# A hybrid decoder layer on one core: the forms of h made at later tiles, and the last group's output stores issued by SP

## Chip, cores and metric

One core of one Trainium2 chip. The metric is the device time of one execution in microseconds. Before the change it is 947.24 us, the median of 3 runs (946.95 to 947.94).

## What is computed

One decoder layer over 512 tokens of width 2048, in float32:

```python
h = rms_norm(x, norm_gain)
z = h @ w_in
q, k, v, g_attn, c_b, c_c, c_h, g_conv = split(z)
y_attn = sliding_window_attention(rope(norm(q)), rope(norm(k)), v, sinks) * silu(g_attn)
y_conv = c_b * short_conv(c_c * c_h, conv_w) * silu(g_conv)
x = x + concat(y_attn, y_conv) @ w_out
gate = sigmoid(rms_norm(x, ple_gate_norm_gain) @ w_ple_gate + b_ple_gate)
e = rms_norm(p @ w_ple_proj, ple_norm_gain)
return x + gate * e
```

Attention has 16 query heads and 4 key heads of 64, in blocks of 128 tokens; the convolution has three taps.

## The kernel before, in words

Every float32 operand of a matmul is split into an upper part (a cast to fp32r on ACT) and the remainder (a subtraction on DVE), and each product is made of three matmuls: upper by upper, remainder by upper, upper by remainder (`mm3`, L154; names end in h and l).

**First stage.** k and v come first (L268 to L284), from 16 tiles of x as they arrive. Then `product` (L514) is called for tiles numbered from 0: tiles 0 to 7 are q, tiles 8 to 14 alternate c and h of the convolution (8 c, 9 h, 10 c, 11 h, 12 c, 13 h, 14 c); one last h tile follows at L1283. A tile is one `gemm_tile` (L165): 16 steps k of three matmuls each, with a weight split fetched every four. After every second k it calls `tick` (L144), which runs what was set with `at(when, ...)` for that count. So the small PE work (sums over heads, transposes, attention's scores, transposes and values) is put between the matmuls at fixed places: `token_rstd` (L233) puts the sum of x's squares at c0+3, the transposes of its copy (`take_rows`, L208, the tile rowsum; `to_tokens`, L213) at c0+5, and the spreading of the result rb at c0+8, c0 being the start of tile 0; the sums of k's squares stand at c0+6, and those of q tile t mostly six ticks after its end. Tiles 2 to 5 also hold an `e_block` (L543), the projection of p, in their middle. Attention's 16 cells are spread over tiles 6 to 14.

In this stage only PE's order is the code's own (L53). The orders of ACT, DVE, POOL and SP are chosen when the kernel is built, from the program's order and estimated times; each of them then runs in that fixed order. The tiles tagged "big" (31 buffers) hold x, squares, rotated heads, rowsum, and the tiles of the forms.

**The forms of h.** The second stage multiplies 2 x 2 blocks by sums of blocks, a scheme of seven products per block. `h_forms(j)` (L646), for j from 0 to 7, makes for the pair of tiles 2j, 2j+1 of h those sums that are not plain blocks: it loads two tiles of x again (L650, through SP; the tile xg), scales each by the norm gain on ACT (L651), makes four half-width sums on DVE (L604, L605, L611, L612; the tile g), splits them with ACT and DVE (L585, L586; the tiles hf) and stores the four results to DRAM through POOL's queue (L654; h_dram). In the second stage `bring` (L1313) loads them back through SP. `load_p` (L533) loads p and splits it (ptsh, ptsl) ahead of tile 0.

`busy` maps a tile's number to functions that `product` calls after that tile's matmuls have been issued (L519). Before the change, `h_forms(0)` is called ahead of tile 0 and `h_forms(1)` to `h_forms(7)` after the tiles 0, 1, 2, 3, 6, 9 and 12.

**Later stages.** Eight groups g of 28 steps on PE, each step 12 matmuls at L854. Here the orders of all engines are the code's own (L706): `soon(before | after, s, fn)` hangs work on a step. The weights of the first steps (wx, wy, loaded by `load_more`, L765, through SP) use the room of the "big" tiles, so their loads wait for these. Groups 6 and 7 are the gate. In `gate_group` (L1152), `finish(t, n, s)` (L1198) puts the sigmoid after step s, the product with e and the accumulating load of x2 (`add_x2`, L1192, through POOL) after s + 1, and `store` (L1195) after s + 5: the output of 128 x 2 x 512 values, 512 KB, through POOL's queue. In group 7 two quarters go this way, (0, 1) with the store after step s0 + 25 and (1, 1) after s0 + 26; the other two are stored in pieces of 256 and 128 KB by `piece` (L1239), through SP, from step s0 + 25 to the end.

Of the kernel before, what the change touches and what calls it, by code (L numbers as in the profile page):

```python
# [30 lines left out]
def f32(ap):  # L31
    return ap.bitcast(F32)
# [3 lines left out]
def hymba_layer(ctx: ExitStack, tc: tile.TileContext, io):  # L36
# [14 lines left out]
    nc = tc.nc  # L51
# [253 lines left out]
    with ExitStack() as att:  # L305
# [218 lines left out]
        def btile(name):  # L524
            return big.tile([P, T], F32, tag="big", name=name)
# [7 lines left out]
        def load_p():  # L533
            load_pg(0)
            for k in range(2):
                pt = btile("pt")
                nc.gpsimd.dma_start(pt, io["p"][k])
                pts.append(split_tile(pt, name="pts"))
# [107 lines left out]
        def h_forms(j):  # L646
            raw = []
            for k in (2 * j, 2 * j + 1):
                raw.append(btile("xg"))
                nc.sync.dma_start(raw[-1], io["x"][k])  # L650
                nc.scalar.activation(raw[-1], raw[-1], AF.Copy, scale=norm_g[:, k : k + 1])  # L651
            _, work = make_forms(
                raw, lambda: btile("g"), lambda: (None, big.tile([P, 2, 2 * P], F32R, tag="big", name="hf")),
                sink=lambda i, t: nc.gpsimd.dma_start(h_dram[j][i], f32(t.rearrange("p a b -> p (a b)"))),  # L654
            )
            for piece in ("g57", "g63", "5", "63", "7"):
                work[piece]()

        load_p()
        h_forms(0)  # L660
        for j, i in enumerate((0, 1, 2, 3, 6, 9, 12), 1):
            busy.setdefault(i, []).append(lambda j=j: h_forms(j))
        for u in range(NKV * NB):
            attention(u // NB, u % NB, c0 + (51 + 7 * u if u < 2 else 65 + 46 * (u - 2) // 13))
# [80 lines left out]
    for g in range(NG):  # L745
        w, n = groups[g]
# [313 lines left out]
    def part(ap, t, n):  # L1060
        return ap[:, 2 * t : 2 * t + 2, n * T : (n + 1) * T]
# [88 lines left out]
    out = io["out"].rearrange("b p n -> p b n")  # L1150

    def gate_group(g):  # L1152
        s0 = g * PER
        q, ext = {}, {}
# [38 lines left out]
            nc.gpsimd.dma_start(q[t, n], x2_dram[t][2 * (g - 6) + n], accum_op=ALU.add)  # L1193

        def store(t, n):  # L1195
            nc.gpsimd.dma_start(part(out, t, 2 * (g - 6) + n), q[t, n])

        def finish(t, n, s):  # L1198
            soon(after, s, sigmoid, t, n)
            for b in range(2):  # L1200
                soon(after, s + 1, times_e, t, n, b)
            soon(after, s + 1, add_x2, t, n)
            soon(after, s + 5, store, t, n)
# [192 lines left out]
def build(arrays):  # L1396
    import concourse.bacc as bacc

    nc = bacc.Bacc("TRN2", target_bir_lowering=False, num_devices=1)
    io = {  # L1400
        n: nc.dram_tensor(f"in_{n}", v.shape, mybir.dt.from_np(v.dtype), kind="ExternalInput").ap()
        for n, v in arrays.items()
    }
    io["out"] = nc.dram_tensor("out_t", (NB, P, D), F32, kind="ExternalOutput").ap()
    with tile.TileContext(nc) as tc:
        hymba_layer(tc, io)
    return nc
# [9 lines left out]
```

## Time and profile before

| what | value |
|---|---|
| median of 3 runs | 947.24 us |
| the profiled execution | 947.18 us |
| its span, first to last instruction | 945.4 us |
| PE busy | 924.7 us (98%) |
| DVE busy | 740.2 us (78%) |
| ACT busy | 535.8 us (57%) |
| POOL busy | 147.4 us (16%) |
| mean granted TensorE clock | 0.992 |

The profile is one execution recorded on the chip. PE is TensorE's matmuls and PEld its weight loads, DVE is VectorE, ACT ScalarE, POOL GpSimd, SP SyncE, which issues DMAs. In rows in order of time the columns are the start and the duration in us, engine, line, operation, output <- inputs and the count; a bracket gives the time that the engine sat idle before it and what it waited for. Matmuls are pipelined, so their starts, not their durations, tell the rate. In tables by stretches PEclk is the granted clock as a share of full speed.

### The profile page before, as it was taken

Reading aid. Unit: us, or ns where it says so; the run is one execution under the profiler, and the core shown is the slowest. Engines: PE = TensorE matmul, PEld = TensorE weight load, DVE = VectorE, ACT = ScalarE, POOL = GpSimd, SP = SyncE. Lnnn points to the kernel's source line nnn. Section 1 sums busy time; section 2 is a strip of 40 time slices with the busy share of each in tenths; the row PEclk is TensorE's granted clock in tenths of the full one; section 3 lists DMA queues with packets and bytes.
Section 4 is the critical chain, followed back from the end, with each engine's and each line's share of the span. In section 5 each row is a group of like instructions: output and inputs, shape, how many; then the busy total and the mean of one; then the engine's idle time right before and its main releaser. Section 6 shows DMA issues by size and latency. Waiting matters only on the chain.

```text
span 945.4 us, 12287 instructions
## 1 busy us (share of the span) xinstructions
PE 924.7 (98%) x4264; PEld 767.8 (81%) x4264; DVE 740.2 (78%) x1115; ACT 535.8 (57%) x890; POOL 147.4 (16%) x192
## 2 busy tenths in 40 slices
PE   9959999999999999999999999999999999999997
PEld 8848878888888888888888888888888888888885
DVE  6756898897786667677767778989767796999778
ACT  7634766777775344445444436655566676575452
POOL 2012224134232000100100020010120112001101
PEclk9979999999999999999999999999999999999999
DMA  8543676436567866734933888794996996578747
GB/s 313 178 153 134 222 245 210 135 92 162 109 179 229 303 223 192 166 108 148 255 90 131 238 237 240 246 265 110 282 346 198 223 282 164 133 228 271 180 135 211
DMA packets 68334, 188.22 MB, mean 199 GB/s; under 512 B 8144, under 2 KB 14592, under 8 KB 68272
## 3 DMA queue, kind: packets, MB, share of 16 engines
q1 hardware_dynamic: 46768, 129.52, 40.1%
q0 software_dynamic: 21360, 57.91, 26.6%
q8 instruction: 33, 0.54, 0.2%
q14 instruction: 29, 0.24, 0.1%
q10 hardware_dynamic: 144, 0.01, 0.0%
HBM read 158.05 MB, written 29.36 MB: 198 GB/s over the span
## 4 chain that ended last, share of the span: by engine, by line
PE 94%; DVE 3%; issue 1%; DMA 1%; ACT 1%; SPq 0%; DVEq 0%; ACTq 0%
PE psp L854 59%; PE psg L155 6%; PE psg L156 6%; PE psg L157 6%; PE pst L854 3%; PE pss L276 2%; PE pst L276 2%; PE pst L920 2%; PE pst L484 1%; PE pss L564 1%; PE pst L564 1%; PE pss L452 1%; PE pss L451 1%; PE pso L499 1%; PE pso L498 1%
## 5 line engine op out<-in xcount | busy, mean ns | idle before, releaser
L854 PE MATMUL psp<-wh,form 128*128 128x512 f32 x1152 | 356.2, 390 | 0.0
L854 PEld LDWEIGHTS psp<-wh,form 128*128 128x128 f32 x1152 | 215.3, 188 | 44.4 <-DVE form L586 0.4
L854 PE MATMUL psp<-wl,form 128*128 128x512 f32 x576 | 224.2, 389 | 0.0
L821 DVE TENSOR_TENSOR wl<-wy,wh 128x1024 fp32r<-128x1024 f32 x96 | 117.1, 1221 | 53.1 <-ACT wh L820 52.3
L820 ACT CAST wh<-wy 128x1024 fp32r<-128x1024 f32 x96 | 100.8, 1051 | 92.5 <-PE psp L854 72.7
L854 PEld LDWEIGHTS psp<-wl,form 128*128 128x128 f32 x576 | 108.1, 188 | 22.5
L820 ACT CAST wh<-ws 128x1024 fp32r<-128x1024 f32 x64 | 67.5, 1054 | 71.4 <-PE psp L854 48.5
L821 DVE TENSOR_TENSOR wl<-wx,wh 128x1024 fp32r<-128x1024 f32 x64 | 78.3, 1223 | 37.3 <-ACT wh L820 36.9
L820 ACT CAST wh<-wx 128x1024 fp32r<-128x1024 f32 x64 | 67.4, 1052 | 69.4 <-PE psp L854 59.2
L155 PE MATMUL psg<-hsh,wh 128*128 128x512 f32 x256 | 103.1, 403 | 0.0
L156 PE MATMUL psg<-hsl,wh 128*128 128x512 f32 x256 | 100.7, 393 | 0.0
L157 PE MATMUL psg<-hsh,wl 128*128 128x512 f32 x256 | 100.4, 392 | 0.0
L854 PE MATMUL psp<-wh,hsh 128*128 128x512 f32 x256 | 100.0, 391 | 0.0
L854 PE MATMUL psp<-wl,hsh 128*128 128x512 f32 x256 | 99.6, 389 | 0.0
L854 PE MATMUL psp<-wh,hsl 128*128 128x512 f32 x256 | 99.6, 389 | 0.0
L821 DVE TENSOR_TENSOR wl<-ws,wh 128x1024 fp32r<-128x1024 f32 x64 | 78.2, 1222 | 27.0 <-ACT wh L820 26.9
L118 DVE TENSOR_TENSOR wl<-raw,wh 128x512 fp32r<-128x512 f32 x88 | 60.2, 686 | 27.4 <-ACT wh L117 11.2
L806 DVE TENSOR_TENSOR wy<-wy,ws 128x1024 f32<-128x1024 f32 x64 | 77.9, 1217 | 0.0
L117 ACT CAST wh<-raw 128x512 fp32r<-128x512 f32 x88 | 54.1, 616 | 41.7 <-PE psg L156 29.4
L157 PEld LDWEIGHTS psg<-hsh,wl 128*128 128x128 f32 x256 | 48.5, 189 | 10.6
L854 PEld LDWEIGHTS psp<-wl,hsh 128*128 128x128 f32 x256 | 48.1, 188 | 9.9
L854 PEld LDWEIGHTS psp<-wh,hsl 128*128 128x128 f32 x256 | 48.1, 188 | 9.9
(232 smaller groups left out, 1401.4 us busy)
## 6 DMA issues: line engine op xcount, KB each, us to landing
raw<-in_w_in SPq DMA_DIRECT2D x32, 512.0 KB, 3.6
ws<-in_w_mid SPq DMA_DIRECT2D x32, 512.0 KB, 4.3
wx<-in_w_mid SPq DMA_DIRECT2D x20, 512.0 KB, 3.7
h<-hf POOLq DMA_DIRECT2D x32, 256.0 KB, 3.4
wy<-in_w_mid SPq DMA_DIRECT2D x16, 512.0 KB, 7.9
wx<-in_w_out SPq DMA_DIRECT2D x16, 512.0 KB, 6.9
ws<-in_w_out SPq DMA_DIRECT2D x16, 512.0 KB, 5.9
ws<-in_w_ple_gate SPq DMA_DIRECT2D x16, 512.0 KB, 4.4
```

Source lines behind the costliest of these rows:

```text
L117: nc.scalar.copy(wh, raw)
L118: nc.vector.tensor_tensor(wl, raw, f32(wh), op=ALU.subtract)
L155: nc.tensor.matmul(ps, wh, ah, start=first, stop=False)
L156: nc.tensor.matmul(ps, wh, al, start=False, stop=False)
L157: nc.tensor.matmul(ps, wl, ah, start=False, stop=last)
L276: nc.tensor.matmul(kv_ps[t], w[:, t, :], a, start=k == 0 and i == 0, stop=k == KT - 1 and i == 2)
L564: nc.tensor.matmul(banks[t], a, w, start=k == 0 and i == 0, stop=k == 1 and i == 2)
L806: tt(y, y, got[g, "s1" if f == 6 else "s0", c], op=ALU.add)
L820: nc.scalar.copy(wh, src)
L821: tt(wl, src, f32(wh), op=ALU.subtract)
L854: nc.tensor.matmul(ps[t], a, w[:, i], start=start and first and i == 0 and n == 0, stop=last and i == 1 and n == 2, skip_group_check=not s ...
L920: nc.tensor.transpose(pt[:, b], quads[b // 2][:, b % 2, f * P : (f + 1) * P], ident)
```

## The change

`h_forms` is no longer called ahead of tile 0; the eight calls come after the tiles 1, 2, 6, 8, 9, 11, 12 and 13 (q's second, third and seventh tile, and five of the convolution's c and h). And in the last group (g = 7) `store` issues its two output stores through SP's queue instead of POOL's; group 6 stays as it was.

```diff
@@ -657,8 +657,7 @@
         load_p()
-        h_forms(0)
-        for j, i in enumerate((0, 1, 2, 3, 6, 9, 12), 1):
+        for j, i in enumerate((1, 2, 6, 8, 9, 11, 12, 13)):
             busy.setdefault(i, []).append(lambda j=j: h_forms(j))
@@ -1193,7 +1192,8 @@
         def store(t, n):
-            nc.gpsimd.dma_start(part(out, t, 2 * (g - 6) + n), q[t, n])
+            engine = nc.gpsimd if g == 6 else nc.sync
+            engine.dma_start(part(out, t, 2 * (g - 6) + n), q[t, n])
```

## Rows read from the trace of the kernel before

**Rows 1.** The page's first part: busy time, share of the span, instructions.

```profile
PE 924.7 (98%) x4264; PEld 767.8 (81%) x4264; DVE 740.2 (78%) x1115; ACT 535.8 (57%) x890; POOL 147.4 (16%) x192
```

**Rows 2.** PE's waits over the whole span: total us, times, longest.

```profile
PE psm L219 <- ACT rowsum L210: 10.6, 1, 10.6
...
PE pso L205 <- ACT sh L130: 1.0, 1, 1.0
PE pss L451 <- DVE negm L459: 0.7, 1, 0.7
```

**Rows 3.** PE in order of time, 56 to 76 us.

```profile
56.70 0.39 PE L157 MATMUL psg<-hsh,wl 128*128 128x512 f32 x1
67.66 0.58 PE L219 MATMUL psm<-ident,rowsum 2*128 2x2 f32 x4 [10.57 <-ACT rowsum L210]
68.17 0.80 PE L155 MATMUL psg<-hsh,wh 128*128 128x512 f32 x1
...
73.46 0.39 PE L157 MATMUL psg<-hsh,wl 128*128 128x512 f32 x1
...
75.54 0.39 PE L157 MATMUL psg<-hsh,wl 128*128 128x512 f32 x1
```

**Rows 4.** By stretches: us, each engine's busy time, PEclk, DMA share, GB/s.

```profile
60.00:62.00 2.00, 0.00 (x0) 0.00 (x0) 0.00 (x0) 0.00 (x0) 0.00 (x0) 0.50 0.96 363
```

**Rows 5.** ACT in order of time, 56 to 68 us.

```profile
56.05 1.14 ACT L130 CAST ptsh<-pt 128x512 fp32r<-128x512 f32 x2
62.80 0.72 ACT L651 ACTIVATE xg<-xg,norm_gain 128x512 f32<-128x512 f32 x1 [5.61 <-DMA xg<-in_x]
...
67.04 0.57 ACT L210 COPY rowsum<-pso 2x512 f32<-2x512 f32 x1
```

**Rows 6.** SP's issues in order of time: the first four loads of xg.

```profile
58.70 1.85 SPq L650 DMA_DIRECT2D xg<-in_x  x4
```

**Rows 7.** DVE in order of time, 58 to 71 us.

```profile
58.22 1.28 DVE L131 TENSOR_TENSOR ptsl<-pt,ptsh 128x512 fp32r<-128x512 f32 x2
...
68.28 0.17 DVE L243 TENSOR_REDUCE ms<-psm 128x4 f32<-128x8 f32 x1 [0.40 <-PE psm L219]
...
70.03 0.43 DVE L249 COPY rb<-r_x 128x512 f32<-128x512 f32 x1 [1.38 <-POOL r_x L229]
```

**Rows 8.** Groups by line: one of the four sums; the subtractions of all sets.

```profile
L605 DVE TENSOR_TENSOR g<-xg 128x256 f32<-128x256 f32 x8 | 3.4, 422 | 4.4 <-ACT xg L651 4.4
...
L586 DVE TENSOR_TENSOR hf<-g,hf 128x256 fp32r<-128x256 f32 (+1 forms) x24 | 11.6, 510 | 1.6 <-ACT hf L585 1.4
```

**Rows 9.** By stretches: length, then PE, PEld, DVE, ACT, POOL busy, PEclk.

```profile
134.30:154.30 20.00, 18.64 (x85) 14.66 (x84) 18.77 (x35) 13.73 (x31) 7.15 (x9) 1.00 0.60 210
...
196.00:301.00 105.00, 105.00 (x561) 89.25 (x560) 83.05 (x253) 78.36 (x224) 34.31 (x40) 1.00 0.62 167
```

**Rows 10.** ACT in order of time: after tile 1, and after tile 3.

```profile
94.17 1.33 ACT L651 ACTIVATE xg<-xg,norm_gain 128x512 f32<-128x512 f32 x2
...
132.39 0.72 ACT L651 ACTIVATE xg<-xg,norm_gain 128x512 f32<-128x512 f32 x1 [0.46 <-DMA xg<-in_x]
...
137.72 0.61 ACT L130 CAST sh<-sqh 128x512 fp32r<-128x512 f32 x1
```

**Rows 11.** Ahead of the second stage: POOL, SP and ACT in order of time.

```profile
268.50 0.54 POOL L654 DMA_DIRECT2D h<-hf  x1 [0.53 <-DVE hf L586]
...
285.23 1.82 SPq L778 DMA_DIRECT2D wx<-in_w_mid  x4
...
297.65 1.06 ACT L820 CAST wh<-wx 128x1024 fp32r<-128x1024 f32 x1
```

**Rows 12.** The end: POOL's last store, SP's last, and DMA issues (median us to landing).

```profile
936.43 0.74 POOL L1196 DMA_DIRECT2D out_t<-z  x1 [2.98 <-DMA z<-x]
...
941.76 0.33 SPq L1244 DMA_DIRECT2D out_t<-z  x1
...
out_t<-z POOLq DMA_DIRECT2D x2, 512.0 KB, 4.9
```

## The prediction, made before the changed kernel was run

> **What bounds the kernel now.** I read the page's busy times first: PE is busy 924.7 us of a span of 945.4 [rows 1], so only what makes PE stop, or run slowly, is worth anything. The list of PE's waits comes next. In all the span it names few: 10.6 us once, for the copy rowsum at L210, and 1.0 and 0.7 us for a half of a square and for attention's negated maxima [rows 2]. I then read PE's order of time around the long one. The matmul that starts at 56.70 is the last before the gap; the transposes of rowsum start at 67.66 with 10.57 us of idle ahead of them, and the matmuls that follow are slow: from 68.17 to 73.46 there are 12 starts in 5.29 us, while from 73.46 to 75.54 nine take 2.08, or 0.231 each [rows 3]. The table by stretches says why: the granted clock is 0.50 at 60 to 62 us, the lower of the two levels, 1.2 instead of 2.4 GHz, after PE had been idle from 57.1 on [rows 4]. So the stall costs 10.57 us and, after it, 5.29 - 12 x 0.231 = 2.5 us of half clock.
>
> What made rowsum late is in ACT's order of time: two casts ptsh from 56.05 to 57.19, then nothing for 5.61 us until an xg has come by DMA, then the xg scalings and hf casts of the first h_forms, and behind them rowsum at 67.04 [rows 5]. The product that rowsum copies had been issued on PE before 56.70. The xg loads left SP only at 58.70 [rows 6]. ACT takes its instructions in order, so a copy that could have run was held by the forms of h, which nobody needs before the second stage.
>
> **The change, part by part.**
>
> Taken away ahead of the first q tile: h_forms(0), with its two loads, ACT, DVE and POOL work. The ptsh casts end at 57.19 and rowsum follows, since every other cast that could come ahead of it waits for PE's later matmuls, and those stand behind rowsum's transposes. Rowsum then ends at 57.19 + 0.57 (its own row) = 57.8 less some 0.1 of overlap, and the transposes start at about 57.7 instead of 67.66; PE is ready at 57.1 [rows 3, 5]. Left of the stall: 0.55 us. Gain: 10.57 - 0.55 = 10.0. A gap of half a microsecond comes far short of what the clock fell after, so the 2.5 us of half clock go too.
>
> What is late next: DVE's chain behind those transposes. DVE has the two ptsl until 59.50, then the sum ms; from ms at 68.28 to the end of rb at 70.46 it took 2.2 us, POOL's power between them [rows 7]. In the new order rb is ready at 59.4 + 2.2 = 61.6. PE wants it after 22 more matmuls (six of k 10 and 11, four of sum_k, twelve of k 12 to 15), at 58.0 + 22 x 0.231 = 63.1. Room of 1.5 us: cost 0.
>
> Before, five sets stood early, at the start and after tiles 0 to 3. Two are left there, 0 and 1 after tiles 1 and 2, where a set stood before as well. Each set issues on DVE four half-width sums of 0.42 us and three subtractions, 11.6 us over eight sets in all or 1.45 each: 3.1 us [rows 8]; on SP two loads and on POOL four stores. The set after tile 3 has a price in the trace: its xg was scaled at 132.39 after a wait for DMA, the square's upper half sh came only at 137.72 behind it on ACT [rows 10], PE waited for it [rows 2], and PE was busy 18.64 of 20.00 us in that stretch [rows 9]. With that set gone I take all of 20.00 - 18.64 = 1.36 us as gain; bounds 0 and 1.4.
>
> The set after tile 6 remains in place, so the 0.7 us wait for the maxima stays, bounds 0 and 0.7 of gain. The sets after tiles 9 and 12 had counterparts before. New are those after tiles 8, 11 and 13: 3 x 3.1 = 9.4 us more for DVE between 196 and 301. There PE was busy 105.00 of 105.00 us, with two sets in it, and DVE 83.05, so 22 us were free [rows 9]. What hides the new sets is that free time. I take 0, since two sets in that very stretch cost PE nothing; upper bound 0.7 for each new set, the nearest wait of PE behind DVE [rows 2], 2.1 in all. With the cover gone altogether it is a rival, below. POOL's stores of h move past a<-up, SP's loads past the fetches of raw; both counterparts did so without a wait of PE, cost 0.
>
> The stores of the last group, two of 512 KB, leave POOL's queue for SP's. POOL's second was issued at 936.43 after the wait for its accumulation and landed 4.9 us on, at 941.3; the last small store left SP at 941.76 [rows 12]. On SP the same wait ends at 936.4, and the next store in its order is one whose inputs come over 2 us later, so nothing queues. The end is set by the last small store. Cost 0, bounds -0.7 (the two issues were no load on the end, a gain that only the drain of POOL could give) and +1.3 (a part of the store's 4.9 us before the last store).
>
> The Trainium skill ("DMA: Bandwidth & Descriptors", section on queues, rings and completion order) speaks against this move: it says that each DMA engine takes one queue's descriptors in ring order but turns between queues, so small stores on SP's queue would stand behind the large ones. By that rule the term is anything up to what of 4.9 us is left at 941.76, which by the rows is nothing.
>
> **The sum.** 10.0 + 2.5 + 1.36 = 13.9 us of gain. The profiled execution took 947.18 us (span 945.4) and the median is 947.24, the same within 0.1: 947.24 - 13.9 = 933.4.
>
> **Rivals.**
>
> 1. The stall moves with the set. Set 0 after tile 1 may hold ACT for its xg as it did at 57 us. The worst is the same wait again, 5.61 us on ACT [rows 5], all of it handed to PE's next sum, and the half clock of 2.5 after it: 933.4 + 8.1 = 941.5; half of it, 937.5. For it: SP's loads are again behind fetches that wait. Against it: set 2 stood at that place before and its xg at 94.17 had no wait at all [rows 10].
>
> 2. DVE in c's tiles. If the three new sets find no free slots their 9.4 us go on PE's path: 942.8. For it: the instructions run in one fixed order, and free time counts only where it falls. Against it: 22 us free [rows 9].
>
> 3. Nothing happens: something else on ACT holds rowsum until 67. Then only 1.4 us move, 945.9, or none, 947.2. The waits show no other candidate.
>
> 4. Slower, by the start of the second stage. SP's loads of wx take the room of the freed tiles and left at 285.23, when attention's last tiles came free; the last set's store was issued at 268.50, and ACT's first cast of wx ran at 297.65 [rows 11]. The last set now belongs to tile 13 instead of 12, one tile or about 15 us later (105 us hold some seven tiles [rows 9]): 268.5 + 15 and up to 4.9 to land, as 512 KB took [rows 12], is about 288, while the cast has 297.65 - 285.23 = 12.4 us less 4.9 for its load, so 7.5 us of room. It decides from a store landed after about 293. To lose more than the 13.9 us it would have to come after 309, behind the last tile: some 16 us of wait and 2.5 of half clock, 933.4 + 18.5 = 952. Against it: the set of tile 12 ran ahead of its tile, since it needs only x.
>
> 5. The large store, on SP's queue, delays the last small ones by all its 4.9 us [rows 12]: 938.3. For it only that its issue might slip; the rows put 5.3 us between the two. The page named above would have it so if they met.
>
> **How the numbers follow.** Forecast 0.71; rival 1 0.10, rival 2 0.07, rival 5 0.04, rival 3 0.03 (of it 0.02 within the bound), rival 4 0.05. The forecast's own bounds: lowest, with the 0.55 and the wait of 0.7 gone too and 0.7 at the end, 933.4 - 2.0 = 931.4; highest, with the 1.36 kept, 2.1 in c's tiles and 1.3 at the end, 938.1. The range takes in rival 5 and the smaller half of rival 1: 931.4 to 939.0, which leaves out 2 in 10. A measurement of this kernel can tell some 0.2%, 1.9 us, from no change. Faster by more: 0.71 + 0.10 + 0.07 + 0.04 + 0.01 = 0.93; within it 0.02; slower 0.05.
>
> **What would show it.** Right: PE's wait for rowsum at L210 falls from 10.6 to under 1 us, no stretch between 50 and 80 us has a clock below 0.9, the wait for sh is gone, PE is busy in nearly all of c's stretch, and the second stage starts some 14 us earlier. Then the tail from PE's end to the span's end is unchanged. Wrong: a new wait of PE of some microseconds for sh, prob or ptl between tiles 1 and 14 (rivals 1, 2), ACT waiting for wx ahead of the second stage (rival 4), or out_t stores of SP landing later (rival 5).

## The result, and the profile after

The changed kernel took **939.68 us** (median of four runs, 936.5 to 940.46) against 947.35 (946.95 to 947.94) for the kernel before, measured beside it: a ratio of 0.9912, 95% interval 0.9889 to 0.9936. The forecast was 933.4, its range 931.4 to 939.0. The direction was right and the size was not: 7.7 us came of the 13.9 that were summed. Line numbers from L660 to the store are lower by one in the changed kernel; from L1196 on they agree again.

Where the gain was expected, it came. PE's waits over the whole span, total, times and longest, now read (answering [rows 2]):

```profile
PE psp L853 <- DVE wl L820: 3.4, 1, 3.4
...
PE pss L451 <- DVE negm L459: 0.7, 1, 0.7
PE psm L219 <- ACT rowsum L210: 0.6, 1, 0.6
```

The wait for rowsum fell from 10.6 to 0.6 us, the wait for sh is gone, the 0.7 for the maxima stayed. The 3.4 us at the top are new. By stretches (length, PE busy, granted clock, DMA share, GB/s), answering [rows 4, 9]:

```profile
49.60:80.40 30.80, 30.18 (x139) 1.00 0.31 104
134.30:154.30 20.00, 20.00 (x94) 1.00 0.48 159
196.00:301.00 105.00, 105.00 (x544) 1.00 0.71 205
300.00:320.00 20.00, 16.62 (x74) 1.00 0.93 337
```

No half clock is left behind the old stall, and PE is as busy in c's tiles as before, with five sets in them. The loss that shows is in the last row, at the start of the second stage. ACT and DVE around the old stall, in order of time (answering [rows 5, 7]):

```profile
57.23 0.57 ACT L210 COPY rowsum<-pso 2x512 f32<-2x512 f32 x1
79.82 0.73 ACT L651 ACTIVATE xg<-xg,norm_gain 128x512 f32<-128x512 f32 x1 [3.43 <-DMA xg<-in_x]
```
```profile
59.57 0.15 DVE L243 TENSOR_REDUCE ms<-psm 128x4 f32<-128x8 f32 x1
61.09 0.43 DVE L249 COPY rb<-r_x 128x512 f32<-128x512 f32 x1 [1.17 <-POOL r_x L229]
```

Rowsum ends at 57.80, rb at 61.5; set 0 did hold ACT for 3.43 us in its new place, and PE has no wait there.

Now the start of the second stage. First the kernel before: PE's first product of the stage, POOL's last accumulating store of attention's output, and the vector operation that makes u for the last convolution.

```profile
312.81 0.39 PE L854 MATMUL psp<-wh,hsh 128*128 128x512 f32 x1
...
306.49 1.02 POOL L504 DMA_DIRECT2D a<-up  x1 [2.45 <-DMA a<-up]
...
313.01 0.69 DVE L1288 TENSOR_TENSOR u<-psg,zc 128x512 f32<-128x512 f32 x1 [7.75 <-PE psg L157]
```

The same in the changed kernel, with what DVE does behind u and the PE instruction that waited:

```profile
299.44 0.39 PE L853 MATMUL psp<-wh,hsh 128*128 128x512 f32 x1
...
277.79 0.66 POOL L503 DMA_DIRECT2D a<-up  x1 [0.70 <-ACT up L501]
...
288.66 1.07 POOL L504 DMA_DIRECT2D a<-up  x1 [8.10 <-issue]
...
297.44 1.03 POOL L504 DMA_DIRECT2D a<-up  x1 [2.31 <-DMA a<-up]
...
305.35 0.69 DVE L1288 TENSOR_TENSOR u<-psg,zc 128x512 f32<-128x512 f32 x1 [10.61 <-DMA a<-up]
...
308.05 2.35 DVE L801 TENSOR_TENSOR wy<-wy,wx 128x1024 f32<-128x1024 f32 x2
310.32 1.22 DVE L820 TENSOR_TENSOR wl<-wx,wh 128x1024 fp32r<-128x1024 f32 x1
...
311.59 0.50 PE L853 MATMUL psp<-wl,hsh 128*128 128x512 f32 x1 [3.38 <-DVE wl L820]
```

Read this from the bottom. PE wants a half of a weight form, wl, which is in DVE's queue behind the sums wy, the convolution and u. Before, u started 0.20 us after the stage's first product, as soon as PE had finished its input. Now it starts 5.91 us after it (305.35 - 299.44), and not for PE but for a DMA of `a<-up`, a transfer whose data u does not use.

The reason is the room in SBUF. The buffers of zc and up rotate over four places, and u, allocated once that pool's work is done, lies partly over one of them. The addresses in the two builds show which: before, the last tile in that place was a zc, left by DVE long ago; in the changed kernel, where the sets stand at other tiles, the rotation comes out differently and the last tile there is the last up, attention's last output. So u is held until the store of that output has finished.

The spans agree with this: the stage starts 312.81 - 299.44 = 13.4 us earlier and the new wait takes 3.4, which leaves 10.0, while the two spans differ by 945.4 - 934.7 = 10.7. The other 0.7 is, within 0.1, at the end: from the start of PE's last product to the span's end it was 7.15 us before and is 6.39 now (the stores, below). That profiled execution, at 936.5 us, was the fastest of the four; the other three took 3 to 4 us more.

The end (answering [rows 12]), SP's last large store and last small ones:

```profile
927.02 0.38 SPq L1196 DMA_DIRECT2D out_t<-z  x1
929.17 3.01 SPq L1244 DMA_DIRECT2D out_t<-z  x3
```

### The profile page after: what moved, and what is told of

Its sections match the earlier page's. It is cut to its first block, busy times and chain, and to the rows that moved or that the text cites. A ratio compares the mean times of both kernels' runs of the same rounds, so it can differ in the third digit from the quotient of the medians.

```text
span 934.7 us, 12298 instructions
## 1 busy us (share of the span) xinstructions
PE 922.9 (99%) x4264; PEld 765.9 (82%) x4264; DVE 737.3 (79%) x1115; ACT 533.5 (57%) x890; POOL 145.8 (16%) x190
## 4 chain that ended last, share of the span: by engine, by line
PE 96%; DVE 2%; issue 1%; ACT 0%; DVEq 0%
PE psp L853 60%; PE psg L155 6%; PE psg L156 6%; PE psg L157 6%; PE pst L853 3%; PE pss L276 2%; PE pst L276 2%; PE pst L919 2%; PE pst L484 1%; PE pss L564 1%; PE pst L564 1%; PE pss L451 1%; PE pss L452 1%; PE pso L499 1%; PE pso L498 1%
```

## The experiments

Three theories stood: A, u's wait for the store; B, the transfers at 270 to 310 us crowd each other, whatever u's buffer, because the last set's stores and loads now fall there; C, the sets in c's tiles hold DVE up. Two notes on the texts on record: they count tiles from one ("behind tile 14" is number 13 in the code, the stall ahead of PE's transposes of rowsum is called the stall behind tile 1, and the seventh run's "two sets behind tile 2" are the two after number 0), and that of the fifth run speaks of two sets where its edit moves three. The edits shown are against the changed kernel, its stores included, unless the kernel before is named. All times below are medians; the first four runs were on one chip, where the kernel before took 947.0 us beside them, the other four on another, where it took 946.56.

**The changed kernel again.**

> The changed kernel itself, unchanged, for a profile of one of its usual executions: the profiled one took 936.5 us, the other three 939.4 to 940.5. Theory A (the first vector operation of the second stage, which makes u, waits for the store of attention's last output, because u's buffer lies over that output's) expects 939 to 940 us, and in the profile a wait of u for that store again, ending later than the 305.35 us of the first profile by about the difference of the two spans, so up to 309; the time of the second stage's start and its end-to-end length otherwise as before. Theory B (attention's transfers and the second stage's loads crowd each other at 270 to 310 us, whatever u's buffer) expects the same time, but the extra 3 us in loads (wx, wy, wl) rather than behind u. Theory C (the sets in c's tiles hold up VectorE) expects new waits of TensorE for VectorE between 200 and 300 us.

Measured: 935.87 us (six runs, 933.39 to 940.98), ratio 0.9887, interval 0.9867 to 0.9906. The kernel scatters by 7.6 us where the one before has 2.4. The profiled execution was the slowest, 940.98 us, and that is what makes it useful. PE, DVE, and PE by stretches:

```profile
301.08 0.39 PE L853 MATMUL psp<-wh,hsh 128*128 128x512 f32 x1
...
313.26 0.80 PE L853 MATMUL psp<-wl,hsh 128*128 128x512 f32 x1 [3.40 <-DVE wl L820]
```
```profile
307.01 0.69 DVE L1288 TENSOR_TENSOR u<-psg,zc 128x512 f32<-128x512 f32 x1 [10.18 <-DMA a<-up]
```
```profile
312.00:314.00 2.00, 0.74 (x2) 0.65 1.05 387
314.00:316.00 2.00, 2.00 (x7) 0.50 1.04 400
316.00:318.00 2.00, 2.00 (x6) 0.50 1.05 387
318.00:320.00 2.00, 2.00 (x7) 0.64 0.52 187
320.00:322.00 2.00, 2.00 (x11) 1.00 0.00 0
```

u is again 5.93 us behind the first product and PE's wait again 3.40 us; what differs is that the clock went to 0.50, the lower level (1.2 GHz), behind it. From the matmul that had waited to the span's end it is 939.2 - 313.26 = 625.9 us here and 934.7 - 311.59 = 623.1 in the first profile: 2.8 us of half clock. The other 1.6 us were lost before the stage began. Theory A's wait is there; the extra microseconds were not in it, as A's text had it, but ahead of it and in the clock after it.

**u written over zc in place.**

```diff
-    u, y = itile("u"), rowp.tile([P, T], F32, tag="rows", name="yconv")
+    u, y = zc, rowp.tile([P, T], F32, tag="rows", name="yconv")
```

> The changed kernel with u written over zc in place, so that u has no buffer of its own and waits for no store. Theory A expects 933 to 935 us: the 3.4 us of TensorE's wait for wl in the profiled execution and the some 3 us more of the usual ones come back, 939.7 - 5.6 = 934.1. Theory B expects 937 to 940 us, with TensorE waiting for another operand at the second stage's start for as long as it did for wl. Theory C expects 939 to 940 us, no change.

Measured: 932.45 us (931.93 to 935.72), ratio 0.9853, interval 0.9840 to 0.9866. The operation starts when PE lets it, and PE does not stop; the stage's first product, DVE, then the stretch at the stage's start:

```profile
302.17 0.39 PE L853 MATMUL psp<-wh,hsh 128*128 128x512 f32 x1
...
302.37 0.69 DVE L1288 TENSOR_TENSOR zc<-psg,zc 128x512 f32<-128x512 f32 x1 [5.87 <-PE psg L157]
```
```profile
300.00:320.00 20.00, 20.00 (x90) 1.00 0.95 341
```

The DMA engines are as crowded as in the changed kernel (0.95 and 341 GB/s against 0.93 and 337), so crowding by itself costs nothing here: B in its simple form falls, and so does C as the cause of this loss. But the profiled execution, at 935.72 the slowest of four, shows what C is about. SP, ACT, PE's waits, and the stretches after (length, then PE, PEld, DVE, ACT and POOL busy, granted clock, DMA share, GB/s):

```profile
210.38 1.44 SPq L650 DMA_DIRECT2D xg<-in_x  x1
```
```profile
218.28 0.72 ACT L651 ACTIVATE xg<-xg,norm_gain 128x512 f32<-128x512 f32 x1 [3.75 <-DMA xg<-in_x]
```
```profile
PE pso L498 <- ACT pth_a L489: 1.6, 1, 1.6
```
```profile
216.00:226.00 10.00, 8.23 (x41) 6.31 (x40) 6.06 (x17) 6.70 (x18) 4.01 (x6) 0.93 0.50 120
226.00:236.00 10.00, 10.00 (x49) 8.56 (x48) 8.40 (x30) 8.60 (x29) 3.46 (x5) 0.90 0.64 171
```

Of the set after tile 8, the second load reached ACT 7.9 us after its issue (210.38 to 218.28); ACT waited 3.75 us with attention's casts queued behind, PE 1.6 and 0.2 us, and the clock fell for a while. Together they moved the second stage's start to 302.17. The same load was late in the other two profiles of these places: ACT had it 7.1 us after its issue in the run before this one and waited 2.9 us, and 5.6 us after it in the first profile, with 1.4 us of waiting. What that cost PE is in the table of leads below.

**Only the first set moved, beside the next one.**

```diff
-        for j, i in enumerate((1, 2, 6, 8, 9, 11, 12, 13)):
+        for j, i in enumerate((0, 0, 1, 2, 3, 6, 9, 12)):
```

> The changed kernel with only the first set moved: it goes beside the second set of before, after the first tile, and the other seven stay at their places of before; u then comes to lie over a buffer that VectorE left early. Theory A expects the stall behind tile 1 gone (10.0 + 2.5 us), the wait for sh behind the set after tile 3 back (1.4 us), and no wait of u for a store: 947.35 - 12.5 = 934.9, between 934 and 936.5 us. Theory B expects the same up to 300 us and a second stage that starts as freely as before's, since the last set is not at tile 13: also 934 to 937 us, so this run alone does not part A from B. Theory C expects the same as A. A time near 939 us would speak against all three: the gain of moving the first set would then be smaller than the sum says.

Measured: 941.87 us (940.67 to 943.59), ratio 0.9947, interval 0.9935 to 0.9959: no theory had that. ACT, PE, and a stretch (length, then PE, PEld, DVE, ACT and POOL busy, granted clock, DMA share, GB/s):

```profile
70.13 1.33 ACT L651 ACTIVATE xg<-xg,norm_gain 128x512 f32<-128x512 f32 x2
...
76.55 0.62 ACT L130 CAST sh<-sqh 128x512 fp32r<-128x512 f32 x1
```
```profile
77.22 0.80 PE L205 MATMUL pso<-sh,ind 128*128 128x512 f32 x1 [4.75 <-ACT sh L130]
```
```profile
78.00:80.00 2.00, 1.96 (x6) 1.57 (x6) 1.97 (x4) 0.00 (x0) 0.00 (x0) 0.50 0.92 340
```

With two sets in one tile, ACT comes to the next square's upper half sh only at 76.55, and PE waits 4.75 us for it, with the half clock behind. It has the form of the wait of the set after tile 3 [rows 2, 10], 1.0 us there, made larger. At the second stage's start, u came 0.20 us after the first product, over a buffer that DVE had left.

**The stores alone.** The kernel before with `engine = nc.gpsimd if g == 6 else nc.sync` in the last group's store, as in the change's second part.

> The kernel before with only the last group's stores put through SP's queue. All theories expect the time of before within 0.5 us (947.35, so 946.8 to 947.9). Rival: the 512 KB store ahead of the small ones on SP's queue holds the last of them up, 948 to 952 us.

Measured: 946.32 us (eleven runs), ratio 0.9991, interval 0.9982 to 1.0. A gain of 0.7 us at the edge of what can be told, half a microsecond below what the theories had expected; no loss, so the rival is out. The end agrees: from the start of PE's last product to the span's end it is 6.41 us in this profile against 7.15 before.

**The last three sets one tile earlier.**

```diff
-        for j, i in enumerate((1, 2, 6, 8, 9, 11, 12, 13)):
+        for j, i in enumerate((1, 2, 6, 8, 9, 10, 11, 12)):
```

> The changed kernel with the last two sets one tile earlier (behind tiles 11 and 13 instead of 12 and 14), so that the last set's transfers are out of the way of the second stage's first loads; u's buffer is still the one of attention's last output. Theory A (u's wait for that output's store sets the loss) expects the wait to stay unless the store itself lands before TensorE's last product of c, about 299.5 us: TensorE's stall at the second stage's start as before, 2 to 4 us with or without the half clock behind it, 935 to 939.5 us. Theory B (the last set behind tile 14 crowds the transfers of the second stage's start) expects the stall gone: 932 to 934 us.

Measured: 932.18 us (931.75 to 934.43), ratio 0.9854, interval 0.9840 to 0.9868. PE, POOL, DVE and SP:

```profile
300.04 0.39 PE L853 MATMUL psp<-wh,hsh 128*128 128x512 f32 x1
```
```profile
276.63 0.66 POOL L503 DMA_DIRECT2D a<-up  x1 [2.29 <-ACT up L501]
...
284.68 1.08 POOL L504 DMA_DIRECT2D a<-up  x1 [5.29 <-issue]
...
293.86 1.03 POOL L504 DMA_DIRECT2D a<-up  x1 [2.43 <-DMA a<-up]
```
```profile
302.52 0.69 DVE L1288 TENSOR_TENSOR u<-psg,zc 128x512 f32<-128x512 f32 x1 [10.03 <-DMA a<-up]
```
```profile
205.64 0.91 SPq L650 DMA_DIRECT2D xg<-in_x  x2
```

A had expected the loss to stay, and it is gone, though u still waits for the store by name. The store was issued 6.2 us ahead of the stage's first product instead of 2.0, u came 2.48 us after that product instead of 5.91, and PE had no wait for wl. So A was half of it: the buffer makes u wait, and the last set's place makes what it waits for late. Undoing either mends it. The edit did one more thing: SP's order, chosen when the kernel is built, now has both loads of the set after tile 8 together (205.64), where in the changed kernel a fetch stood between them and the second left 6.4 us after the first. So this run and the next also lack the late load, and their medians do not part the two effects; the rows at the second stage's start do.

**Both.** The same tiles, and u over zc.

> The same, with u written over zc besides. Theory A expects 932 to 933.5 us, the time of the run with u over zc alone (932.45), since the last set's place then no longer matters. Theory B expects the same 932 to 934 us as with the last set's place alone changed. The two theories part on the difference of the two runs: 3 to 6 us for A, none for B.

Measured: 932.67 us (932.05 to 933.16), ratio 0.9856, interval 0.9841 to 0.9871, the same as each alone: no difference to the fifth run, as B's text had it, because that run had already won back all there was. It has the narrowest scatter, and its profile has no wait of PE above 1.1 us.

**One set in each of the first five tiles.**

```diff
-        for j, i in enumerate((1, 2, 6, 8, 9, 11, 12, 13)):
+        for j, i in enumerate((0, 1, 2, 3, 4, 6, 9, 12)):
```

> One set in each of the tiles after the first five, then the places of before (so the first stage has one set per tile and no two in one); u lies over a buffer that VectorE left early; stores of the last group through SP's queue. If the sum's first two terms are right (10.0 us of the stall behind tile 1 and 2.5 us of half clock) and the loss of the run with two sets behind tile 2 was only the 4.8 us wait for sh and the half clock behind that, 947.0 - 12.5 = 934.5 us, less 0.7 for the stores: 933.5 to 935.5 us, with a wait for sh of 1 to 2 us. A wait for sh of 4 us or more would put it at 939 to 942 us again and say that q's early tiles have no room for a set at all.

Measured: 935.55 us (935.04 to 936.2), ratio 0.9885, interval 0.9872 to 0.9899, just above the range expected. PE's waits:

```profile
PE pso L205 <- ACT sh L130: 1.0, 1, 1.0
PE pss L276 <- ACT wh L117: 1.0, 1, 1.0
```

So most of the loss of the run with two sets in one tile was the pairing. The thinning out of q's early tiles is worth some 935.55 - 932.2 = 3.3 us against the best runs, more than the 1.36 us that was summed for it; but that sum was against the kernel before, and here a set stands after tile 4 too. The wait for sh is the one of the kernel before; that for wh has nothing to do with the sets, it falls at 6.14 us, at the kernel's start. The table of leads below parts the two sizes.

**The kernel before, with u over attention's last output.**

```diff
+    pads = [itile("pad") for _ in range(2)]
+    for pad in pads:
+        nc.vector.memset(pad[:, :1], 0.0)
     u, y = itile("u"), rowp.tile([P, T], F32, tag="rows", name="yconv")
...
     last_conv()
+    for pad in pads:
+        nc.vector.memset(pad[:, :1], 0.0)
```

> The kernel before, with two small buffers put in front of u so that u comes to lie over attention's last output, as it does in the changed kernel. There the last store is issued at 306.5 us, 6.5 us ahead of the end of c's last tile, against 2.0 us in the changed kernel. Theory A in its full form (the buffer makes the wait, the store's lateness makes its price) expects u to wait for the store by name but to end within 1 us of 313: 947.0 to 948 us. If the buffer alone made the loss, 950 to 953 us.

Measured: 947.23 us (eleven runs), ratio 1.0007, interval 0.9998 to 1.0016. PE, POOL, DVE and PE's wait:

```profile
312.46 0.39 PE L854 MATMUL psp<-wh,hsh 128*128 128x512 f32 x1
```
```profile
305.97 1.03 POOL L504 DMA_DIRECT2D a<-up  x1 [2.32 <-DMA a<-up]
```
```profile
315.17 0.06 DVE L1287 MEMSET pad<- 128x1 f32 x1 [10.26 <-DMA a<-up]
315.34 0.69 DVE L1291 TENSOR_TENSOR u<-psg,zc 128x512 f32<-128x512 f32 x1
```
```profile
PE psp L854 <- DVE wl L821: 0.4, 1, 0.4
```

The store was issued 6.5 us ahead of the stage's first product (312.46); the second pad, which lies over a part of that output too, already waited for it, u came 2.88 us after the product (later than A's text had it), and PE paid 0.4 us. The buffer alone costs next to nothing. Four profiles now lie on one line, u's start behind the first product against PE's wait for wl:

```
before                        0.20 us   0
last three sets earlier       2.48      0
before, u over the last up    2.88      0.4
changed kernel                5.91      3.4
```

In these profiles some 2.5 us of DVE's delay are free, and beyond that each microsecond is PE's.

## Why the prediction was right or wrong

**The terms that were summed held.** The 10.0 us of the stall: PE's wait fell from 10.57 to 0.6, rowsum ended at the forecast 57.8, and rb at 61.5 against 61.6, with no wait of PE for it, so that chain cost nothing. The 2.5 us of half clock went with it. The 1.36 us went, and were somewhat undersized, as the leads show: how much earlier the same PE instruction starts than in the profile before, in us.

```
start before, and what it is      changed  again   u over zc  last earlier  both   first five
 84.99  sums of a q tile (L205)    12.44   12.65    12.60       12.69      12.50    12.39
162.37  sums of a later q tile     14.25   13.18    14.72       12.77      14.18    12.39
250.87  attention's values (L498)  13.76   11.76    10.64       12.77      14.18    11.27
312.81  second stage, product 1    13.37   11.73    10.64       12.77      14.18    11.27
334.57  second stage, product 97    9.65    5.15    10.64       12.53      14.18    11.27
```

The columns are the changed kernel's two profiles and the second, fifth, sixth and seventh runs. The first row is the stall and its half clock, 12.5 summed. In the columns "changed" and "both" the second row adds 1.7 to 1.8 us, where 1.36 was summed; with a set left after tile 3 it adds nothing, and the one after tile 4 goes with another 1.1 lost by the third row. ("Again" and "last earlier" lost 1.1 and 1.6 us between the first two rows, in tile 3, where PE waited 0.6 us for a remainder wl at L564; why in those profiles is open.) Against the kernel before, the three mended kernels (932.18 and 932.67 beside 946.56, 932.45 beside 947.0) gained 13.9 to 14.6 us where the sum had 13.9; some 0.7 of that is the stores, which the sum had at 0, with a gain of up to 0.7 in its bounds.

**The step that failed** is "New are those after tiles 8, 11 and 13 ... I take 0, since two sets in that very stretch cost PE nothing". It priced the later sets by DVE's free time in c's tiles alone, and PE did stay busy there in the first profile. Most of the price came behind the stretch: a set after tile 13 makes attention's last store late, and u waits for it. It measured 3.4 us of PE's wait, with 2.8 of half clock behind it in one profile of two; the bound for all new sets was 2.1. With these two the forecast would be 933.4 + 3.4 + 2.8 = 939.6, beside the 939.68 measured, but none of the three executions near that was profiled. The set after tile 8 belongs to this step too: from the second to the third row of the table the lead falls by 0.5, 1.4 and 4.1 us in the three profiles that have its loads apart, and not at all in the two that have them together. "POOL's stores of h move past a<-up ... cost 0" failed with it: it looked for a wait of PE beside those stores, and the late store's price fell one stage on.

**Rival 4** had the place, the start of the second stage, and the last set's place as the reason, but the wrong mechanism: it looked at ACT's wx casts, which PE never waited for. Nothing in it asked which buffers come to lie where once the order of the work changes. The rotation could not be read from the trace of before, but the question could have been put: each tile allocated behind a rotating pool has some last holder, and moving work may change who that is.

**Rival 1** was right that ACT would wait for set 0's load, 3.43 of the feared 5.61 us, and right in neither price: PE had no wait there. **Rival 2** did not occur as a whole; single late loads did. **Rivals 3 and 5** fell. For rival 5, the last large store left SP at 927.02 and landed some 5 us on, while the last small ones left from 929.17 to 932.2: they met in part, the end got shorter (7.15 to 6.39 us), and the store's move alone measured 0.9991, no loss. The rule of the Trainium skill ("DMA: Bandwidth & Descriptors", the section on queues, rings and completion order) was tried only in so far as they met, and no run here shows the delay that it would give.

**The range.** Its upper end had no case for this loss, and the first measurement missed it by 0.7 us; the repeated one, 935.87, lies in it. Why three of the first four executions were at 939.4 to 940.5 and most of the later ones at 933.4 to 937.4 is not settled: the profile of 940.98 us has the half clock behind the wait, that of 936.5 us has not, and no more were taken. The mean granted clock on record goes with it: 0.995 to 0.997 in the five executions of 937.38 us and more, 0.997 to 0.999 in the five below. A difference of 0.003 over 938 us is some 2.8 us (an estimate from these numbers). The clock is not all of it: 933.39 and 934.46 lie less than 3.4 us above the mended kernels' fastest, 931.75, so the wait itself was probably shorter there. The Trainium skill ("TensorE: Matmul & The Clock Gate", Part 1, the HAM clock gate) says of a kernel's start that the number of slow matmuls varies from run to run of the same kernel. Here the like shows in the middle of one: the waits of 3.38 and 3.40 us are equal, and the clock behind them is 1.00 and 0.50.

What made the last store late in itself was shown only by moving the sets. In the changed kernel the first store in question (the first half of the last output but two) was issued 21.7 us ahead of the stage and POOL's next one of attention's output came 10.9 us later (277.79 to 288.66); with the sets a tile earlier it was 23.4 us ahead and 8.1 later (276.63 to 284.68). That the wx and wy loads in the same stretch lengthen its landing was argued from their times, and not tried apart.

## What to carry to other kernels

Where work is moved, look past the stretch that it is moved into, at the first thing that has to wait for its end: a late store holds a buffer, and a tile that was allocated over that buffer holds its engine's whole queue, though it shares no data with it. A wait on a DMA whose output the instruction doesn't read is the sign of it in a trace. Two halves that are harmless alone can make one loss; undo them one at a time, and where possible also add one alone to the kernel before.

## What was not expected of the hardware

The store of attention's last output, 128 KB, held its buffer for 7.9 to 9.2 us after its issue in the profiles where u or a pad waited for it (297.44 to 305.35, 305.97 to 315.17), with the DMA engines' share at 0.93 and 0.97 in those stretches, where the median of such stores from issue to landing, in the changed kernel between 280 and 307 us, was 3.8. And where SP's issue of the second load of the set after tile 8 took 1.44 and 1.65 us, ACT had that load 7.9 and 7.1 us after the issue; in the third profile with the changed kernel's places the issue took 0.38 us and ACT had the load 5.6 us after it.
